# The down projection of a two-layer MLP by the seven-product form of the 2x2 block product

## The chip, the cores and the metric

The kernel runs on one core of one Trainium2 chip, as one launch. The metric is the device time of an execution in microseconds (us), the median of the runs.

## The reference

One transformer block on 256 tokens of width 1024, in float32. Attention comes first and is untouched by this change; it ends in a projection and a residual. Then comes the part that the change is about, a feed-forward block with a hidden width of 4096 (cut to what matters):

```python
def squared_relu_mlp(x, w_up, w_down):          # x 256x1024, w_up 1024x4096, w_down 4096x1024
    return jnp.square(jax.nn.relu(x @ w_up)) @ w_down

def reference(x, ...):
    h = x
    u = moba_attention(rms_norm(h, norm_mix_pre[0]), attn_w_qkv[0], attn_w_o[0])
    h = h + rms_norm(u, norm_mix_post[0])
    u = squared_relu_mlp(rms_norm(h, norm_ffn_pre[0]), w_up[0], w_down[0])
    return h + rms_norm(u, norm_ffn_post[0])
```

## The kernel before

**Split operands.** TensorE multiplies in a format (float32r) that keeps part of a float32's bits. So every operand is split exactly into a high part and a low part, and `mm3` (L209 to L214) issues three matmuls for each product: high by high, high by low, low by high. For weights the split is made on chip by the class `Weights`: ScalarE (ACT) copies a slice of the loaded `raw` tile to `hi` (L83), and VectorE (DVE) subtracts, `lo = raw - hi` (L84), with both inputs in SBUF. A few of these subtractions, outside the feed-forward block's steady part, are given to GpSimd (POOL).

**The stream of weights.** A piece is a tile of 128 x 2048 (1 MB); five raw tiles and four pairs of parts are in flight. `pump(n)` issues the next n splits (512 columns each) of a fixed list `steps`; `get` makes sure that a split needed by a matmul has been issued; `done` releases parts. When the last split of a piece has been issued, the load of a later piece is put on SyncE's (SP) queue. The order of PE and SP is the order of the program text; ACT, DVE and POOL are ordered by a list scheduler by priority, outside sections marked as manual, and each engine then runs its instructions in that fixed order.

**The feed-forward block.** The hidden width is cut into eight chunks of 512. The first chunk goes by token tiles, while the residual's norm is worked out (`up_first`). Every later chunk c is `up_chunk(c)`: four groups f of 128 hidden units, each 8 x 3 matmuls of 256 columns (tokens) into one PSUM bank `psu`; then `up_evac`: DVE takes relu times the norm to `r` (L555), ACT squares it twice, to `uhi` (L556) and `u` (L557), and DVE subtracts `ulo = u - uhi` (L558). After `up_chunk(c)` comes `down_chunk(c-1)`: 4 row blocks x 2 token tiles x 2 column halves x 3 = 48 matmuls of 512 columns into four accumulator banks `acd` that stay open over all chunks. The last chunk's down products are done by output tile, so that `PostNorm` (square on ACT, a power on POOL, the gain and the residual on DVE, L526 to L533) overlaps the next tile's matmuls.

PSUM is eight banks: pool `mm` has four (the accumulators), pool `at` four (the `psu` tiles).

Of the kernel before, what the change touches and what calls it, by code (L numbers as in the profile page):

```python
# [17 lines left out]
P = 128  # L18
# [3 lines left out]


# [4 lines left out]
class Weights:  # L28
    """Streams the weights through SBUF in pieces of [128, 2048] and splits each float32
    exactly into two float32r parts: hi (12 bits, rounded) and lo (the rest). A piece is split  # L30
    in four steps; step (i, j) is the j-th of piece i."""

    N = 2048

    def __init__(self, nc, raw_pool, part_pool, raw_bufs, part_bufs):
        self.nc, self.raw_pool, self.part_pool = nc, raw_pool, part_pool
        self.raw_bufs, self.part_bufs = raw_bufs, part_bufs
        self.sources, self.raw, self.parts, self.steps, self.split = [], {}, {}, [], set()
        self.loaded = self.finished = self.next = self.part = 0
# [23 lines left out]
    def slice(self, t, i, j):  # L63
        how = self.sources[i][1]
        if how == "cols":
            return t[:, :, j * P:(j + 1) * P]
        if how == "rows":
            return t[:, j // 2, (j % 2) * 512:(j % 2) * 512 + 512]
        return t[:, j, :]

    def pump(self, n, lo_engine=None):
        nc = self.nc
        while n > 0 and self.next < len(self.steps):
            i, j = self.steps[self.next]
            if i >= self.finished + self.part_bufs or i >= self.loaded:
                return
            if i not in self.parts:
                shape = list(self.raw[i].shape)
                self.parts[i] = [self.part_pool.tile(shape, F32R, name=f"w{p}{i}", tag=f"w{p}", bufs=self.part_bufs)
                                 for p in ("hi", "lo")]  # L80
            hi, lo = (self.slice(t, i, j) for t in self.parts[i])
            x = self.slice(self.raw[i], i, j)
            nc.scalar.activation(hi, x, AF.Copy)  # L83
            (lo_engine or nc.vector).tensor_tensor(lo, x, f32(hi), op=ALU.subtract)  # L84
            self.split.add((i, j))
            self.next += 1
            n -= 1
            if sum((i, q) in self.split for q in range(4)) == 4:
                self.load()

    def get(self, i, j):
        while (i, j) not in self.split:
# [3 lines left out]
        return self.parts[i]  # L96
# [6 lines left out]
def block(ctx: ExitStack, tc: tile.TileContext, x, g_mix_pre, g_mix_post, g_ffn_pre, g_ffn_post,  # L103
# [20 lines left out]
    # ---- the weights in the order of their use  # L124
# [7 lines left out]
    def add_cols(name, w, c, how, cuts=1):  # L132
        """512 columns in two pieces of four row blocks"""
# [7 lines left out]
    def add_rows(name, w, k):  # L141
        """four row blocks in two pieces"""
# [12 lines left out]
    NC = F // 512  # L155
    for c in range(NC):
        add_cols(f"up{c}", wu, 512 * c, "cols" if c else "k")
        if c > 0:
            add_rows(f"down{c - 1}", wd, 4 * (c - 1))
    add_rows(f"down{NC - 1}", wd, 4 * (NC - 1))  # L160

    # ---- loads: x's columns as the first weights need them
# [21 lines left out]
    # ---- constants  # L184
# [8 lines left out]
    # distances of queries 128.. to keys 0..255, then of queries 0.. to keys 0..127  # L193
    dist = const.tile([P, 384], F32, name="dist")
# [12 lines left out]
    oT = [const.tile([P, HEADS, S], F32R, name=f"oT{i}") for i in range(2)]  # L207
# [26 lines left out]
    def diag_of(rstd):  # L234
        """diagonal matrices of rstd, split in two parts"""
# [7 lines left out]
    def row_of(dg, dst, pool):  # L243
        """dst[:, t] = rstd[t] on every partition"""
# [5 lines left out]
    # ---- x transposed, times the first gain; its rows' norms come in later  # L250
# [20 lines left out]

    qk_pool = tc.alloc_tile_pool(name="qk_pool", bufs=1)
# [71 lines left out]
    # ---- attention, a head at a time; the queries of the second half come first  # L344
# [60 lines left out]
    # ---- values, queries and keys of the first heads  # L405
# [3 lines left out]
    def keep_busy(n):  # L409
        """products of zeros, which keep TensorE's clock up while it waits"""  # L410
# [73 lines left out]
    # ---- projection of the heads' outputs  # L484
# [60 lines left out]
    rrow2 = const.tile([P, S], F32, name="rrow2")  # L545
    up = {}

    def up_tiles(c):
        up[c] = [mlp.tile([P, 4, S], F32R, name=f"u{p}") for p in ("hi", "lo")]

    def up_evac(c, f, ps):
        hi, lo = (a[:, f, :] for a in up[c])
        r = mlp.tile([P, S], F32, name="r")
        u = mlp.tile([P, S], F32, name="u")
        nc.vector.scalar_tensor_tensor(r, ps[:, :S], 0.0, rrow2, op0=ALU.max, op1=ALU.mult)  # L555
        nc.scalar.activation(hi, r, AF.Square)  # L556
        nc.scalar.activation(u, r, AF.Square)  # L557
        nc.vector.tensor_tensor(lo, u, f32(hi), op=ALU.subtract)  # L558
# [11 lines left out]
    def up_first_relu(t):  # L570
        r = mlp.tile([P, 512], F32, name=f"r0_{t}", bufs=1)
        nc.vector.tensor_scalar(r, rT[t], rstd2[:, t:t + 1], 0.0, op0=ALU.mult, op1=ALU.max)
        rT[t] = r

    def up_first_evac(t):
# [3 lines left out]
        hi, lo = (a[:, :, t * P:(t + 1) * P] for a in up[0])  # L579
        u = mlp.tile([P, 4, P], F32, name=f"u0_{t}", bufs=1)  # L580
        psv = ps.rearrange("p (f c) -> p f c", c=P)
        nc.scalar.activation(hi, psv, AF.Square)
        nc.scalar.activation(u, psv, AF.Square)
        nc.vector.tensor_tensor(lo, u, f32(hi), op=ALU.subtract)
# [4 lines left out]
    with tc.manual_schedule(engines=ELEMENTWISE):  # L589
# [20 lines left out]
        up_tiles(0)  # L610
# [15 lines left out]
        for k in range(KT):  # L626
# [10 lines left out]
            if k == 6:  # L637
                row_of(dg, rrow2, at)
# [6 lines left out]
    def up_chunk(c):  # L645
        up_tiles(c)
        for f in range(4):
            ps = bank(at, f"psu{c}_{f}")
# [5 lines left out]
            if f == 3:
                W.done(2)
            W.pump(2)
            up_evac(c, f, ps)

    def down_chunk(c):
        for f in range(4):  # L660
            for t in range(NT):
                for n in range(2):
                    a = [b[:, f, t * P:(t + 1) * P] for b in up[c]]
                    rows_unit(f"down{c}", f, a, t, n, c == 0 and f == 0, False)
            if f % 2:
                W.done(1)
            W.pump(2)

    for c in range(1, NC):
        up_chunk(c)  # L670
        if c == 1:
            acc = [[bank(mm, f"acd{t}_{n}") for n in range(2)] for t in range(NT)]
        down_chunk(c - 1)
    ov = out[0].rearrange("(t p) d -> p t d", p=P)

    def act_down(f, t):
        return [b[:, f, t * P:(t + 1) * P] for b in up[NC - 1]]

    for t in range(NT):
        norm = PostNorm(t, "ffn")  # L680
        for c in range(2):
            last_rows(f"down{NC - 1}", act_down, t, c)
            norm.take(c)
        for a, b in ((0, 512), (512, D)):
            norm.put(yg, a, b)
            nc.sync.dma_start(ov[:, t, a:b], yg[:, t, a:b])
    W.done(2)
# [25 lines left out]
```

## Time and profile before

| what | value |
|---|---|
| time, median of 3 runs | 306.8 us (306.6 to 307.12) |
| span of the profiled execution, first to last instruction | 304.8 us |
| median time less that span | 2.0 us |
| PE busy | 295.1 us (97%) |
| DVE busy | 194.1 us (64%) |
| ACT busy | 166.6 us (55%) |
| POOL busy | 24.4 us (8%) |

The span is from one profiled execution; the time of a run is the device's own and holds 2.0 us that lie around the span. A matmul's duration in the trace is longer than the step from one matmul to the next, since they are pipelined; the cost of a matmul in a dense stream is therefore read from start to start.

### The profile page before, as it was taken

What the parts mean: (1) busy time and instruction counts of PE and PEld (TensorE: products, weight loads), DVE (VectorE), ACT (ScalarE), POOL (GpSimd) and SP (SyncE); (2) the same over time, 40 slices, a digit from 0 to 9 for tenths busy, and PEclk for the clock granted to TensorE, in tenths of its full rate; (3) what the DMA queues carried; (4) which work ended last, traced back from release to release, by engine and by line L of the source; (5) the groups of instructions that cost most, each with busy time, mean ns of one, the idle gap of its engine ahead of it and who ended that gap; (6) DMA issues with size and microseconds to landing.
All of it is one profiled execution on the core that took longest, in us unless ns stands there. A gap on an engine that the chain in (4) does not pass through costs nothing.

```text
span 304.8 us, 4862 instructions
## 1 busy us (share of the span) xinstructions
PE 295.1 (97%) x1838; PEld 261.9 (86%) x1838; DVE 194.1 (64%) x403; ACT 166.6 (55%) x395; POOL 24.4 (8%) x38
## 2 busy tenths in 40 slices
PE   8999999999999989999999999999999999999991
PEld 4689999988998868898898898898898898898880
DVE  3569989774688296899448447447447447547042
ACT  4777938765393365987437427427527526526020
POOL 4000224002200072000000000000000000000000
PEclk9999999999999999999999999999999999999998
DMA  6998694739405234078970860960960950300012
GB/s 201 374 387 310 205 380 172 251 133 347 141 3 166 110 138 140 0 254 293 298 261 1 310 245 0 326 226 2 336 214 9 345 199 12 129 0 3 0 57 80
DMA packets 22055, 53.79 MB, mean 176 GB/s; under 512 B 1024, under 2 KB 1552, under 8 KB 22032
## 3 DMA queue, kind: packets, MB, share of 16 engines
q1 hardware_dynamic: 22032, 53.49, 50.1%
q8 instruction: 14, 0.23, 0.3%
q14 instruction: 9, 0.07, 0.1%
HBM read 52.44 MB, written 1.05 MB: 175 GB/s over the span
## 4 chain that ended last, share of the span: by engine, by line
PE 80%; issue 10%; DVE 5%; DMA 2%; SPq 1%; ACT 1%; POOL 1%; DVEq 0%; POOLq 0%
PE psu L212 10%; PE psu L214 10%; PE psu L213 10%; PE acd L213 9%; PE acd L212 9%; PE acd L214 9%; PE psq L212 3%; PE psq L213 3%; PE psq L214 3%; DVE wlo L84 2%; PE psv L292 2%; PE psv L294 2%; PE psv L296 2%; DMA raw<-in_attn_w_qkv_dram 2%; PE psk L212 1%
## 5 line engine op out<-in xcount | busy, mean ns | idle before, releaser
L84 DVE TENSOR_TENSOR wlo<-raw,whi 128x512 fp32r<-128x512 f32 x182 | 118.3, 697 | 43.2 <-ACT whi L83 43.0
L83 ACT ACTIVATE whi<-raw 128x512 fp32r<-128x512 f32 x192 | 107.0, 623 | 46.4 <-PE acd L214 33.3
L212 PE MATMUL psu<-xT,whi 128*128 128x256 f32 x224 | 63.4, 283 | 0.0
L213 PE MATMUL psu<-xT,whi 128*128 128x256 f32 x224 | 63.3, 282 | 0.0
L214 PE MATMUL psu<-xT,wlo 128*128 128x256 f32 x224 | 62.9, 281 | 0.0
L213 PE MATMUL acd<-wlo,uhi 128*128 128x512 f32 x128 | 50.5, 395 | 0.0
L212 PE MATMUL acd<-whi,uhi 128*128 128x512 f32 x128 | 50.5, 395 | 0.0
L214 PE MATMUL acd<-whi,ulo 128*128 128x512 f32 x128 | 50.5, 394 | 0.0
L214 PEld LDWEIGHTS psu<-xT,wlo 128*128 128x128 f32 x224 | 42.5, 190 | 0.0
L213 PEld LDWEIGHTS psu<-xT,whi 128*128 128x128 f32 x224 | 42.1, 188 | 0.3
L212 PEld LDWEIGHTS psu<-xT,whi 128*128 128x128 f32 x224 | 41.9, 187 | 0.3
L556 ACT ACTIVATE uhi<-r 128x256 fp32r<-128x256 f32 x28 | 11.6, 413 | 35.0 <-DVE r L555 35.0
L214 PEld LDWEIGHTS acd<-whi,ulo 128*128 128x128 f32 x128 | 24.1, 188 | 5.6
L212 PEld LDWEIGHTS acd<-whi,uhi 128*128 128x128 f32 x128 | 24.1, 188 | 5.4
L213 PEld LDWEIGHTS acd<-wlo,uhi 128*128 128x128 f32 x128 | 24.1, 189 | 5.3
L558 DVE TENSOR_TENSOR ulo<-u,uhi 128x256 fp32r<-128x256 f32 x28 | 11.8, 423 | 14.4 <-ACT u L557 14.4
L555 DVE SCALAR_TENSOR_TENSOR r<-psu,rrow 128x256 f32<-128x256 f32 x28 | 11.7, 419 | 13.7 <-PE psu L214 13.7
L212 PE MATMUL psq<-xT,whi 128*128 128x256 f32 x64 | 18.4, 288 | 0.0
L212 PE MATMUL psk<-xT,whi 128*128 128x256 f32 x64 | 18.4, 287 | 0.0
L529 POOL TENSOR_TENSOR rs<-mss,power 128x1 f32<-128x1 f32 x4 | 2.2, 550 | 198.6 <-DVE mss L527 198.6
L214 PE MATMUL psq<-xT,wlo 128*128 128x256 f32 x64 | 18.1, 282 | 0.0
L213 PE MATMUL psq<-xT,whi 128*128 128x256 f32 x64 | 18.0, 282 | 0.0
(121 smaller groups left out, 455.2 us busy)
## 6 DMA issues: line engine op xcount, KB each, us to landing
raw<-in_w_up_dram SPq DMA_DIRECT2D x16, 1024.0 KB, 5.6
raw<-in_w_down_dram SPq DMA_DIRECT2D x16, 1024.0 KB, 7.5
raw<-in_attn_w_qkv_dram SPq DMA_DIRECT2D x10, 1024.0 KB, 8.6
raw<-in_attn_w_o_dram SPq DMA_DIRECT2D x4, 1024.0 KB, 5.7
raw<-in_attn_w_qkv_dram SPq DMA_DIRECT2D x8, 256.0 KB, 6.3
out_dram<-yg SPq DMA_DIRECT2D x4, 256.0 KB, 2.0
xs<-in_x_dram SPq DMA_DIRECT2D x2, 256.0 KB, 4.9
xs<-in_x_dram SPq DMA_DIRECT2D x1, 512.0 KB, 7.1
```

Of the source, the lines that this page charges most:

```text
L83: nc.scalar.activation(hi, x, AF.Copy)
L84: (lo_engine or nc.vector).tensor_tensor(lo, x, f32(hi), op=ALU.subtract)
L212: nc.tensor.matmul(ps, lhsT=a[0], rhs=b[0], start=start, stop=False)
L213: nc.tensor.matmul(ps, lhsT=a[0], rhs=b[1], start=False, stop=False)
L214: nc.tensor.matmul(ps, lhsT=a[1], rhs=b[0], start=False, stop=stop)
L292: nc.tensor.matmul(psv[0][t], lhsT=x0[t], rhs=w[0], start=first, stop=False)
L294: nc.tensor.matmul(psv[0][t], lhsT=x1[t], rhs=w[0], start=False, stop=False)
L296: nc.tensor.matmul(psv[0][t], lhsT=x0[t], rhs=w[1], start=False, stop=last)
L529: nc.gpsimd.tensor_tensor(self.rs, ms, power[:, :1], op=ALU.pow)
L555: nc.vector.scalar_tensor_tensor(r, ps[:, :S], 0.0, rrow2, op0=ALU.max, op1=ALU.mult)
L556: nc.scalar.activation(hi, r, AF.Square)
L558: nc.vector.tensor_tensor(lo, u, f32(hi), op=ALU.subtract)
```

## The change

Only the feed-forward block changes. The hidden width is now taken in 16 pairs q of 2 x 128 rows of `w_down`. For a pair, the two row blocks, the two token tiles and the two 512-column halves make a 2x2 block product. It needs eight block products in the plain form; fifteen of the sixteen pairs now use a seven-product form, whose operands are blocks or sums of blocks. The last pair stays plain. There are seven accumulator banks, `M1` to `M7` (four in `mm`, three in `at`), so one bank of `at` is left for `psu`; both f of a pair share it.

The sums of weights are made on POOL (`add_up`: one subtraction of 1024 columns and two of 512, into one tile `sum` with a single buffer). The sums of activations are made on POOL (`combine`: four operations of 128 columns), on DVE for pair 0. Each down piece then has two units, `blocks` (3 x 512 columns) and `sums` (4 x 512), each split into hi and lo; a split now covers 1024 columns, save one of 512. The activations of a pair are seven 128-column blocks, squared once on ACT, copied to hi by ACT and subtracted to lo by DVE (896 columns each). `down_pair(q-3)` follows `up_pair(q)`. At the end DVE combines the seven banks into four partial results, which the final norm adds to the last pair's products.

```diff
+    def add_up(self, i):
+        raw = self.raw[i]
+        t = self.sums[i] = self.sum_pool.tile([P, 4, 512], F32, name=f"sum{i}", tag="sum", bufs=1)
+        sub = self.nc.gpsimd.tensor_tensor
+        sub(t[:, 0:2, :], raw[:, :, 512:1024], raw[:, 0, :].rearrange("p (h c) -> p h c", c=512), op=ALU.subtract)
+        sub(t[:, 2, :], raw[:, 1, 512:1024], t[:, 0, :], op=ALU.subtract)
+        sub(t[:, 3, :], raw[:, 1, 0:512], t[:, 2, :], op=ALU.subtract)
+
+    def operands(self, u, j):
+        i, kind = self.units[u]
+        raw, (hi, lo) = self.raw[i], self.parts[u]
+        if kind == "blocks":
+            if j == 0:
+                return hi[:, 0, :], lo[:, 0, :], raw[:, 0, 0:512]
+            return hi[:, 1:3, :], lo[:, 1:3, :], raw[:, 1, :].rearrange("p (h c) -> p h c", c=512)
+        if kind == "sums":
+            s = slice(2 * j, 2 * j + 2)
+            return hi[:, s, :], lo[:, s, :], self.sums[i][:, s, :]
+        return tuple(self.slice(t, kind, j) for t in (hi, lo, raw))
...
     def pump(self, n, lo_engine=None):
...
+                if kind == "blocks":
+                    self.add_up(i)
+            hi, lo, x = self.operands(u, j)
             nc.scalar.activation(hi, x, AF.Copy)
             (lo_engine or nc.vector).tensor_tensor(lo, x, f32(hi), op=ALU.subtract)
...
+    for q in range(2, NP):
+        add_pair(q)
+        if q >= LAG:
+            add_down(q - LAG, "seven")
+    for q in range(NP - LAG, NP - 1):
+        add_down(q, "seven")
+    add_down(NP - 1, "rows")
...
+    A21, A11, A22, A12, S1, S3, S2, S4 = range(8)
+    PRODUCTS = (("M1", A11, 0, 0), ("M2", A12, 0, 1), ("M3", S4, 0, 2), ("M5", S1, 1, 0),
+                ("M7", S3, 1, 1), ("M6", S2, 1, 2), ("M4", A22, 1, 3))
...
+    def combine(q):
+        x = hidden.pop(q)
+        if q < NP - 1:
+            tt = (nc.vector if q == 0 else nc.gpsimd).tensor_tensor
+            tt(x[:, S1, :], x[:, A21, :], x[:, A22, :], op=ALU.add)
+            tt(x[:, S3, :], x[:, A11, :], x[:, A21, :], op=ALU.subtract)
+            tt(x[:, S2, :], x[:, S1, :], x[:, A11, :], op=ALU.subtract)
+            tt(x[:, S4, :], x[:, A12, :], x[:, S2, :], op=ALU.subtract)
+        hi, lo = (mlp.tile([P, 7, P], F32R, name=f"u{p}{q}", tag=f"u{p}", bufs=UB) for p in ("hi", "lo"))
+        src, n = (x[:, 1:8, :], 7) if q < NP - 1 else (x[:, 0:4, :], 4)
+        act[q] = hi, lo
+        nc.scalar.activation(hi[:, 0:n, :], src, AF.Copy)
+        nc.vector.tensor_tensor(lo[:, 0:n, :], src, f32(hi[:, 0:n, :]), op=ALU.subtract)
+
+    def up_evac(q, ps):
+        r = mlp.tile([P, 512], F32, name=f"r{q}", tag="r", bufs=2)
+        nc.vector.scalar_tensor_tensor(r, ps, 0.0, rrow2.rearrange("p f s -> p (f s)"), op0=ALU.max, op1=ALU.mult)
+        hidden[q] = r
+
+    def up_finish(q):
+        r = hidden[q]
+        x = hidden_tile(q)
+        nc.scalar.activation(x[:, 0:4, :], r.rearrange("p (f c) -> p f c", c=P), AF.Square)
+        combine(q)
...
-            if k > 1:
+            if k in (2, 4, 6):
                 W.pump(1)
...
+    def up_pair(q):
+        ps = bank(at, f"psu{q}")
+        for f in range(2):
             for k in range(KT):
+                w = [a[:, k, f * P:(f + 1) * P] for a in W.get(piece[f"up{q}"], k // 4)]
+                mm3(ps[:, f * S:(f + 1) * S], w, xk(k), k == 0, k == KT - 1)
+            if q == 2 and f == 1:
                 up_first_evac(1)
+                combine(0)
+                combine(1)
+            if f == 0:
+                W.pump(2)
+        W.done(1)
+        up_evac(q, ps)
+        W.pump(1)
+        up_finish(q)
...
+    def down_pair(q):
+        hi, lo = act.pop(q)
+        if q == 0:
+            for j, (name, *_) in enumerate(PRODUCTS):
+                M[name] = bank(mm if j < 4 else at, f"ac{name}")
+        for name, slot, e, j in PRODUCTS:
+            a = hi[:, slot - 1, :], lo[:, slot - 1, :]
+            w = [b[:, j, :] for b in W.get(piece[f"down{q}"] + e, j // 2)]
+            last = q == NP - 2 and name not in ("M2", "M3", "M4")
+            mm3(M[name], a, w, q == 0, last)
+            if name == "M3":
                 W.done(1)
+            if name in ("M1", "M3", "M6"):
+                W.pump(1)
+        W.done(1)
+
+    for q in range(2, NP):
+        up_pair(q)
+        if q >= LAG:
+            down_pair(q - LAG)
+    for q in range(NP - LAG, NP - 1):
+        down_pair(q)
...
+    nc.scalar.activation(part["m1"], M["M1"], AF.Copy)
+    for d, a, b in (("u2", "M6", "m1"), ("u3", "M7", "u2"), ("u4", "M5", "u2"), ("u7", "M5", "u3")):
+        nc.vector.tensor_tensor(part[d], M[a], part[b], op=ALU.add)
...
+    class FinalNorm(PostNorm):
+        def take(self, c, first):
...
+            nc.vector.tensor_tensor(yc, M[name], yc, op=ALU.add)
...
+            square(scr, yc, ss)
```

LAG is 3 and UB is 2.

## Rows read from the trace of the kernel before

**Rows 1.** The page: engines' busy time, the chain that ended last, granted TensorE clock.
```profile
PE 295.1 (97%) x1838; PEld 261.9 (86%) x1838; DVE 194.1 (64%) x403; ACT 166.6 (55%) x395; POOL 24.4 (8%) x38
...
PEclk9999999999999999999999999999999999999998
...
PE 80%; issue 10%; DVE 5%; DMA 2%; SPq 1%; ACT 1%; POOL 1%; DVEq 0%; POOLq 0%
```

**Rows 2.** Windows: us; busy of PE PEld DVE ACT POOL; clock; DMA share, GB/s.
```profile
127.93:298.40 170.47, 170.45 (x1061) 153.23 (x1059) 98.95 (x184) 84.42 (x180) 0.55 (x1) 1.00 0.45 158
177.08:199.75 22.67, 22.67 (x147) 20.56 (x146) 13.05 (x25) 11.46 (x24) 0.00 (x0) 1.00 0.55 185
```

**Rows 3.** Timeline (start us, us, engine ...) of PE: first matmuls of three stretches.
```profile
127.93 0.28 PE L212 MATMUL psu<-xT,whi 128*128 128x256 f32 x1
...
139.86 0.40 PE L212 MATMUL acd<-whi,uhi 128*128 128x512 f32 x1
...
151.01 0.28 PE L212 MATMUL psu<-xT,whi 128*128 128x256 f32 x1
```

**Rows 4.** Timeline of DVE from 185 us, operations back to back.
```profile
185.73 0.42 DVE L555 SCALAR_TENSOR_TENSOR r<-psu,rrow 128x256 f32<-128x256 f32 x1
186.08 1.29 DVE L84 TENSOR_TENSOR wlo<-raw,whi 128x512 fp32r<-128x512 f32 x2
187.29 0.42 DVE L558 TENSOR_TENSOR ulo<-u,uhi 128x256 fp32r<-128x256 f32 x1
187.63 2.49 DVE L84 TENSOR_TENSOR wlo<-raw,whi 128x512 fp32r<-128x512 f32 x4
```

**Rows 5.** Timeline of ACT from 186 us, operations back to back.
```profile
186.48 0.40 ACT L556 ACTIVATE uhi<-r 128x256 fp32r<-128x256 f32 x1
186.78 0.40 ACT L557 ACTIVATE u<-r 128x256 f32<-128x256 f32 x1
...
190.99 2.19 ACT L83 ACTIVATE whi<-raw 128x512 fp32r<-128x512 f32 x4 [2.25 <-PE acd L214]
```

**Rows 6.** Timeline of DVE, 33 to 41 us, beside POOL's subtractions.
```profile
33.21 1.89 DVE L84 TENSOR_TENSOR wlo<-raw,whi 128x512 fp32r<-128x512 f32 x3
...
35.39 1.79 DVE L84 TENSOR_TENSOR wlo<-raw,whi 128x512 fp32r<-128x512 f32 x1
...
37.44 2.97 DVE L84 TENSOR_TENSOR wlo<-raw,whi 128x512 fp32r<-128x512 f32 x3
```

**Rows 7.** Timeline of POOL, the same stretch.
```profile
35.32 1.30 POOL L84 TENSOR_TENSOR wlo<-raw,whi 128x512 fp32r<-128x512 f32 x1 [12.66 <-ACT whi L83]
37.71 1.55 POOL L84 TENSOR_TENSOR wlo<-raw,whi 128x512 fp32r<-128x512 f32 x1 [1.08 <-ACT whi L83]
```

**Rows 8.** Timeline of DVE and POOL, 109 to 118 us.
```profile
109.07 3.45 DVE L533 SCALAR_TENSOR_TENSOR xs<-yg,rs,xs 128x512 f32<-128x512 f32 x2
117.15 1.41 DVE L533 SCALAR_TENSOR_TENSOR xs<-yg,rs,xs 128x512 f32<-128x512 f32 x2
...
109.01 2.96 POOL L84 TENSOR_TENSOR wlo<-raw,whi 128x512 fp32r<-128x512 f32 x2
```

**Rows 9.** Timeline of DVE at 51.9 us, and of POOL.
```profile
51.94 0.47 DVE L359 SCALAR_TENSOR_TENSOR s<-pss,rstd_q,bias 128x256 f32<-128x256 f32 x1
...
51.98 1.29 POOL L84 TENSOR_TENSOR wlo<-raw,whi 128x512 fp32r<-128x512 f32 x1 [2.11 <-ACT whi L83]
```

**Rows 10.** Timeline of the end, from the last matmul.
```profile
297.98 0.40 PE L214 MATMUL acd<-whi,ulo 128*128 128x512 f32 x1
...
299.33 0.68 DVE L530 TENSOR_TENSOR yg<-acd,g_ffn 128x512 f32<-128x512 f32 x1
299.49 0.55 POOL L529 TENSOR_TENSOR rs<-mss,power 128x1 f32<-128x1 f32 x1 [5.09 <-DVE mss L527]
300.07 1.41 DVE L533 SCALAR_TENSOR_TENSOR yg<-yg,rs,xs 128x512 f32<-128x512 f32 x2
```

**Rows 11.** DMA issues of the up weights, KB each, median us to landing.
```profile
raw<-in_w_up_dram SPq DMA_DIRECT2D x16, 1024.0 KB, 5.6
```

More of the change, by code (lines that the diff above doesn't have):

```diff
@@ L21 @@
 MASKED = 1e30
+UB = 2
+LAG = 3
 def f32(ap):
@@ L33 @@
     N = 2048
+    STEPS = {"cols": 4, "k": 4, "rows": 4, "pair": 2, "blocks": 2, "sums": 2}
     def __init__(self, nc, raw_pool, part_pool, raw_bufs, part_bufs):
@@ L37, in __init__ @@
         self.raw_bufs, self.part_bufs = raw_bufs, part_bufs
-        self.sources, self.raw, self.parts, self.steps, self.split = [], {}, {}, [], set()
+        self.sources, self.raw, self.left = [], {}, []
+        self.units, self.parts, self.steps, self.split = [], {}, [], set()
         self.loaded = self.finished = self.next = self.part = 0
+        self.sum_pool, self.sums = None, {}
     def add(self, src, how, cuts=1):
-        self.sources.append((src, how, cuts))
-        return len(self.sources) - 1
+        kinds = ("blocks", "sums") if how == "seven" else (how,)
+        self.sources.append((src, cuts))
+        self.left.append(sum(self.STEPS[k] for k in kinds))
+        for k in kinds:
+            self.units.append((len(self.sources) - 1, k))
+        return len(self.units) - len(kinds)
     def load(self, n=None):
@@ L61, in load, with slice @@
             self.part = 0
-    def slice(self, t, i, j):
-        how = self.sources[i][1]
-        if how == "cols":
+    def slice(self, t, kind, j):
+        if kind == "cols":
             return t[:, :, j * P:(j + 1) * P]
-        if how == "rows":
+        if kind == "rows":
             return t[:, j // 2, (j % 2) * 512:(j % 2) * 512 + 512]
+        if kind == "pair":
+            return t[:, 4 * j:4 * j + 4, :]
         return t[:, j, :]
+    def add_up(self, i):
[16 more added lines that the diff above has]
+        return tuple(self.slice(t, kind, j) for t in (hi, lo, raw))
     def pump(self, n, lo_engine=None):
@@ L73, in pump, with get @@
         while n > 0 and self.next < len(self.steps):
-            i, j = self.steps[self.next]
-            if i >= self.finished + self.part_bufs or i >= self.loaded:
+            u, j = self.steps[self.next]
+            i, kind = self.units[u]
+            if u >= self.finished + self.part_bufs or i >= self.loaded:
                 return
-            if i not in self.parts:
-                shape = list(self.raw[i].shape)
-                self.parts[i] = [self.part_pool.tile(shape, F32R, name=f"w{p}{i}", tag=f"w{p}", bufs=self.part_bufs)
+            if u not in self.parts:
+                shape = {"blocks": [P, 3, 512], "sums": [P, 4, 512]}.get(kind, list(self.raw[i].shape))
+                self.parts[u] = [self.part_pool.tile(shape, F32R, name=f"w{p}{u}", tag=f"w{p}", bufs=self.part_bufs)
                                  for p in ("hi", "lo")]
-            hi, lo = (self.slice(t, i, j) for t in self.parts[i])
-            x = self.slice(self.raw[i], i, j)
+                if kind == "blocks":
+                    self.add_up(i)
+            hi, lo, x = self.operands(u, j)
             nc.scalar.activation(hi, x, AF.Copy)
             (lo_engine or nc.vector).tensor_tensor(lo, x, f32(hi), op=ALU.subtract)
-            self.split.add((i, j))
+            self.split.add((u, j))
             self.next += 1
             n -= 1
-            if sum((i, q) in self.split for q in range(4)) == 4:
+            self.left[i] -= 1
+            if self.left[i] == 0:
                 self.load()
-    def get(self, i, j):
-        while (i, j) not in self.split:
+    def get(self, u, j):
+        while (u, j) not in self.split:
             n = self.next
@@ L95, in get @@
             assert self.next > n
-        return self.parts[i]
+        return self.parts[u]
     def done(self, n):
@@ L154, in block, with add_pair, add_down @@
     add_rows("o1", wo, 4)
[L155 to L160, printed above, removed]
+    NP = F // 256
+    add_cols("up0", wu, 0, "k")
+    def add_pair(q):
+        i = piece[f"up{q}"] = W.add(wu[:, :, 256 * q:256 * q + 256], "pair")
+        W.steps += [(i, j) for j in range(2)]
+    def add_down(q, how):
+        i = piece[f"down{q}"] = W.add(wd[:, 2 * q:2 * q + 2, :], how)
+        W.steps += [(i, j) for j in range(4)] if how == "rows" else [(i + e, j) for e in range(2) for j in range(2)]
+    for q in range(2, NP):
[5 more added lines that the diff above has]
+    add_down(NP - 1, "rows")
     xs = const.tile([P, NT, D], F32, name="xs")
@@ L206, in block @@
     xT = [const.tile([P, KT, S], F32R, name=f"xT{i}") for i in range(2)]
-    oT = [const.tile([P, HEADS, S], F32R, name=f"oT{i}") for i in range(2)]
+    oT = [o_pool.tile([P, HEADS, S], F32R, name=f"oT{i}") for i in range(2)]
     def mm3(ps, a, b, start, stop):
@@ L511, in block @@
     yg = mlp.tile([P, NT, D], F32, name="yg", bufs=1)
+    W.sum_pool = mlp
     class PostNorm:
@@ L544, in block, with hidden_tile @@
     rstd2 = const.tile([P, NT], F32, name="rstd2")
[L545 to L558, printed above, removed]
+    rrow2 = const.tile([P, 2, S], F32, name="rrow2")
+    A21, A11, A22, A12, S1, S3, S2, S4 = range(8)
+    PRODUCTS = (("M1", A11, 0, 0), ("M2", A12, 0, 1), ("M3", S4, 0, 2), ("M5", S1, 1, 0),
+                ("M7", S3, 1, 1), ("M6", S2, 1, 2), ("M4", A22, 1, 3))
+    hidden, act = {}, {}
+    def hidden_tile(q):
+        hidden[q] = mlp.tile([P, 8, P], F32, name=f"x{q}", tag="x", bufs=2)
+        return hidden[q]
+    @urgent
+    def combine(q):
[11 more added lines that the diff above has]
+        nc.vector.tensor_tensor(lo[:, 0:n, :], src, f32(hi[:, 0:n, :]), op=ALU.subtract)
+    @urgent
+    def up_evac(q, ps):
[7 more added lines that the diff above has]
+        combine(q)
     rT = {}
@@ L578, in up_first_evac @@
             nc.tensor.transpose(ps[:, f * P:(f + 1) * P], rT[t][:, f * P:(f + 1) * P], ident)
[L579 to L584, printed above, removed]
+        for q in range(2):
+            x = hidden[q] if t else hidden_tile(q)
+            psv = ps[:, q * 256:(q + 1) * 256].rearrange("p (f c) -> p f c", c=P)
+            nc.scalar.activation(x[:, 0:4, :].rearrange("p (f t) c -> p f t c", t=2)[:, :, t, :], psv, AF.Square)
     def act_o(f, t):
@@ L637, in block @@
             if k == 6:
-                row_of(dg, rrow2, at)
+                row_of(dg, rrow2[:, 0, :], at)
+                nc.gpsimd.tensor_copy(rrow2[:, 1, :], rrow2[:, 0, :])
             if k % 4 == 3:
                 W.done(1)
-            if k > 1:
+            if k in (2, 4, 6):
                 W.pump(1)
         up_first_relu(1)
[L645 to L648, printed above, removed]
+    o_pool.release()
+    late = ctx.enter_context(tc.tile_pool(name="late", bufs=1, side="right", reuse_waits="tile"))
@@ L653, in up_chunk @@
                 up_first_evac(1)
[L654 to L665, printed above, removed]
-                W.done(1)
[L667 to L673, printed above, removed]
@@ new lines, in block @@
+    M["C22"] = bank(at, "acC22")
+    result = {(0, 0): ("M4", "u3"), (0, 1): ("C22", "u7"), (1, 1): ("M3", "u4"), (1, 0): ("M2", "m1")}
+    hi, lo = act.pop(NP - 1)
+    class FinalNorm(PostNorm):
+        def take(self, c, first):
+            s = slice(c * 512, (c + 1) * 512)
+            name, rest = result[self.t, c]
+            yc = part[rest]
+            nc.vector.tensor_tensor(yc, M[name], yc, op=ALU.add)
+            scr = small.tile([P, 512], BF16, name="scr", bufs=2)
+            ss, ms = self.ss[:, c:c + 1], self.ms[:, c:c + 1]
+            square(scr, yc, ss)
+            nc.vector.tensor_scalar(ms, ss, EPS if first else self.ms[:, 1 - c:2 - c], None, op0=ALU.add)
+            if not first:
+                nc.gpsimd.tensor_tensor(self.rs, ms, power[:, :1], op=ALU.pow)
+            (nc.gpsimd if first or self.t == 0 else nc.vector).tensor_tensor(
+                yg[:, self.t, s], yc, self.gain[:, s], op=ALU.mult)
@@ new lines, in block @@
+    for t in range(NT):
+        norm = FinalNorm(t, "ffn")
+        order = (0, 1) if t == 0 else (1, 0)
+        for n, c in enumerate(order):
+            name = result[t, c][0]
+            for f in range(2):
+                a = [b[:, 2 * f + t, :] for b in (hi, lo)]
+                w = [b[:, f, c * 512:(c + 1) * 512] for b in W.get(piece[f"down{NP - 1}"], 2 * f + c)]
+                mm3(M[name], a, w, f == 0 and name == "C22", f == 1)
+            norm.take(c, n == 0)
+        for c in order:
+            norm.put(yg, c * 512, (c + 1) * 512)
+            nc.sync.dma_start(ov[:, t, c * 512:(c + 1) * 512], yg[:, t, c * 512:(c + 1) * 512])
@@ L691 @@
+    W.done(1)
 _INS = ["x", "norm_mix_pre", "norm_mix_post", "norm_ffn_pre", "norm_ffn_post", "w_up", "w_down",
```

26 lines of the change are left out of this document (8 added, 18 removed).

## The prediction

> **What bounds the kernel now.** I read the page first: PE is busy for 97% of the span and fills 80% of the chain that ended last, DVE is at 64%, ACT at 55%, and POOL, at 8%, is nearly idle; the granted clock is full until the end [rows 1]. So the first guess is that fewer matmuls mean less time. The windows then show the feed-forward block by itself: from 127.93 to 298.40 PE is busy for 170.45 of 170.47 us, and POOL for 0.55 [rows 2]. One chunk of 512 hidden units takes 22.67 us, of which DVE works 13.05 and ACT 11.46 [rows 2]. That leaves DVE some 9.6 us a chunk, or 4.8 a pair. Whether the change fits into that room is the question, and averages over the span don't answer it.
>
> **What it takes from PE.** In the PE timeline the 48 down matmuls of a chunk run from 139.86 to 151.01, so a 512-column matmul costs 11.15 / 48 = 0.2323 us from start to start; the remaining 11.52 us of a 22.67 us chunk are 96 matmuls of 256 columns, 0.120 each [rows 2, 3]. Plain, a pair has 8 x 3 = 24 down matmuls; in the seven-product form 21. Fifteen pairs save 45, or 45 x 0.2323 = 10.45 us. The up matmuls keep their number and shape. A pair then asks of PE 48 x 0.120 + 21 x 0.2323 = 10.64 us, against 11.33 before.
>
> **What it adds to DVE.** Back to back, two 512-column subtractions take 186.08 to 187.29, 0.605 each, and a 256-column operation 185.73 to 186.08, 0.35 [rows 4]. So 256 more columns cost 0.255, and by that line a 1024-column subtraction costs 0.605 + 0.51 = 1.115 and an 896-column one 0.99. Per pair: two up splits 2.23; blocks 0.605 + 1.115 = 1.72; sums 2.23; the activations' lo 0.99; relu of 512 columns 0.605. Together 7.78 us. The upper bound, if the longer operations gain nothing over 512-column ones, is 7040 columns / 512 x 0.605 = 8.32. Alone, DVE would still be done within PE's 10.64.
>
> **ACT.** A 512-column copy costs 2.19 / 4 = 0.55, a 256-column one 0.30 [rows 5], so 1024 columns cost about 1.05 and 896 about 0.92. Per pair five of 1024, one copy and one square of 512, one of 896: 7.3 us, hidden under PE. The copy to a pair's activation parts has to wait for a free buffer (UB is 2) until the down products of two pairs before are done; the weight copies that those products need have to stand ahead of it on ACT, or nothing would move, so I cost that wait at nothing.
>
> **What it adds to POOL, and what that does to DVE.** This is the term that decides. Per pair POOL gets subtractions of 1024, 512 and 512 columns and four of 128, all with both inputs in SBUF. The trace has POOL subtractions of 512 columns: 1.30 us undisturbed [rows 7]. Beside them, look at DVE. Three of its subtractions alone take 1.89 us [rows 6]. The one that starts at 35.39, just behind POOL's of 35.32, takes 1.79 and ends 0.56 us after POOL's end at 36.62. The three from 37.44 take 2.97, and POOL's, issued at 37.71 into the first of them, stretches to 1.55 [rows 6, 7]. From 109.07 two residual operations of DVE (again two SBUF inputs) take 3.45 us beside POOL's; later, without POOL, two take 1.41 [rows 8]. So the two engines take turns: while one runs an operation with two SBUF inputs, the other's waits. A DVE operation with only one input in SBUF, at 51.94, keeps its 0.47 us beside a POOL subtraction [rows 9]; relu, which reads PSUM, is of that kind, the splits aren't. The extra time that one POOL subtraction of 512 columns puts on DVE is 1.79 - 0.61 = 1.18, 2.97 - 1.89 = 1.08, or (3.45 - 1.41) / 2 = 1.02; the mean is 1.09.
>
> The Trainium skill says the same of the mechanism (SBUF — State Buffer, "Who interferes with whom"): a DVE instruction with two SBUF inputs contends with a GpSimd instruction that reads SBUF, and the second to issue blocks until the first is done. By that rule, taken with POOL's whole 1.29 us, the sum below would come to 357 us; by the measured delays it is the lower figure that follows.
>
> No row shows POOL at 1024 columns. I take two times the price of 512 (four units in all, 4 x 1.09 = 4.36 us a pair); at least it is 4 x 1.02, at most POOL's whole time, 4 x 1.29. For 128 columns the bounds are a quarter of 1.02, 0.255, and 0.55, the smallest POOL operation with two tensors that I have (a power on one column) [rows 10]; between them I take 0.40, so 1.6 for four.
>
> So in the steady state DVE needs, working or held up, 7.78 + 4.36 + 1.6 = 13.74 us a pair: more than PE's 10.64, and more than the 11.33 of before. DVE becomes the bound, and PE waits some 3 us in each pair for the lo parts of the sums. Low bound: 4 x 1.02 + 4 x 0.255 = 5.1, with relu run during POOL's turns (7.78 - 0.605), 12.3. High: 8.32 + 4 x 1.29 + 4 x 0.55 = 15.7.
>
> **The sum.** The stretch begins at 127.93, where PE starts the first chunk that goes by column groups [rows 3]. Fifteen pairs of DVE time: 15 x 13.74 = 206.1. Corrections: only 14 up pairs, -2.84; pair 0's activation sums run on DVE (4 x 0.22, by the line above) and not on POOL, -0.73; three up splits are issued before the stretch, -3.35; the last pair's lo, 512 columns, +0.61: -6.3 in all. After the last lo of sums PE still has four products of the last seven-product pair, 12 x 0.2323 = 2.79, and the plain pair, 24 x 0.2323 = 5.58. The end behind the last matmul was 304.8 - 298.4 = 6.4 us, and gets one more DVE addition ahead of the square, 0.68 as its neighbour in that chain [rows 10]: 7.1. Span: 127.93 + 206.1 - 6.3 + 2.79 + 5.58 + 7.1 = 343.2; with the 2.0 that lie between span and median, **345.2 us**. The bounds of a pair's time give 323 and 374. The same formula gives 306.8 at 11.18 us a pair: the change pays only if POOL holds DVE for less than 3.4 us a pair.
>
> **Edits costed at nothing.** The up weights now come in rows of 1 KB and not 2: if that doubled the DMA engines' work on them, the share of 0.55 over a chunk would be 0.83 [rows 2], and a load that lands in 5.6 us [rows 11] has five buffers; covered. The single psu bank has to be emptied during the 4.9 us of down matmuls behind it; one relu of 0.6 fits, even behind one held-up subtraction of 2 to 3.5. The four combining additions on DVE (2.7 us) run under the last 24 matmuls.
>
> **Rivals.**
> - *POOL's work stays off DVE's path.* If these plain float32 sums hold DVE up far less than the splits on POOL did (under 2.9 us a pair), PE stays the bound and the matmuls saved are the result: 306.8 - 10.45 + 0.68 = 297.0 us. For it: PE's 97%, and DVE and POOL each alone fit into 10.64. Against: three separate stretches show the turns, with two kinds of DVE operation. It decides at 3.4 us. Chance 0.15.
> - *Part of the price.* Half of it gives 10.8 us a pair, 301. Chance 0.03.
> - *Waits in fixed queues on top.* `sum` has one buffer, so POOL may start the next pair's sums only after DVE's last lo of this one; then ACT (1.05) and DVE (1.115) follow POOL's last subtraction. If POOL has nothing else in that time, 2.17 us are added to a pair: 15.9, 378 us. Against: `combine` and the up splits can fill it. Chance 0.06.
> - *TensorE's clock falls in the waits.* It stayed at 1.00 through this stretch [rows 2], but PE never waited there. At half clock a pair would take 21.3 us of PE, 458 us; a few slow stretches would vanish in PE's new slack. Chance 0.02.
>
> My own case has the rest, 0.74. Slower by over 0.2% (about what a measurement of this kernel can tell from no change) then is 0.82, faster 0.17, within 0.2% 0.01. The range, 312 to 376, holds my case's bounds of 323 to 374, most of what lies between a partial price and them, and part of the queue rival; together about 0.8.
>
> **What would show it.** In the profile after: DVE's 1024-column subtractions at a mean well above 1.2 us, near 2; POOL busy for some 100 us in the block; DVE's busy share near 1 there; PE's share down to about 83%, its waits put down to DVE's `wlo`; the period of a pair near 13.7 us and the chain led by DVE and POOL. If a pair takes 10.6 us and PE stays dense, the step on POOL's price is wrong.

## The result, and the profile after

The changed kernel takes 337.6 us (median of 4 runs, 337.17 to 338.59) against 306.8: a ratio of 1.100 (95% interval 1.098 to 1.102). Predicted were 345.2 us, 312 to 376. The 45 matmuls fewer did not come back as time: a pair of the down projection now takes 12.7 us, where half a chunk took 11.33.

The page of the changed kernel, the lines of [rows 1]: engines' busy time, granted clock, and the chain that ended last.

```profile
PE 298.6 (89%) x1793; PEld 262.5 (78%) x1793; DVE 286.0 (85%) x356; ACT 187.1 (56%) x342; POOL 204.8 (61%) x143
...
PEclk9999999999999799999599997999799999899595
...
POOL 54%; PE 31%; DVE 8%; issue 3%; ACT 2%; DMA 1%; POOLq 0%; DVEq 0%
```

PE has left the chain's first place to POOL. DVE has fewer instructions than before (356 against 403) and is busy for 92 us more: the instructions themselves have become longer. In part they cover more columns, but the groups by shape (count, then busy us and mean ns) show that this isn't all: a split of 1024 columns takes 2.26 us in the mean where the raw blocks are split, against 1.22 without POOL's sums (the run with all sums on DVE, below).

```profile
L122 DVE TENSOR_TENSOR wlo<-raw,whi 128x1024 fp32r<-128x1024 f32 x43 | 96.1, 2258 | 0.0
L122 DVE TENSOR_TENSOR wlo<-sum,whi 128x1024 fp32r<-128x1024 f32 x30 | 43.5, 1481 | 2.3 <-ACT whi L121 2.3
```

The windows, with columns as in [rows 2], show where: the block's beginning, its steady part, and two single pairs.

```profile
140.00:160.00 20.00, 18.55 (x114) 16.09 (x113) 16.24 (x13) 10.87 (x13) 19.61 (x15) 1.00 0.45 151
...
160.00:260.00 100.00, 89.76 (x543) 80.83 (x544) 100.00 (x65) 55.72 (x64) 98.11 (x57) 0.93 0.54 169
...
199.66:212.38 12.72, 11.89 (x68) 11.09 (x69) 12.72 (x10) 6.96 (x8) 12.48 (x8) 0.87 0.50 167
212.38:225.13 12.75, 11.34 (x71) 9.63 (x70) 12.75 (x9) 6.96 (x8) 12.51 (x8) 1.00 0.53 164
```

From 160 to 260 us DVE and POOL are both busy all the time. Two engines can't both be the bound by their own work; here each one's busy time holds its waiting for the other. The timeline of DVE over one pair of the changed kernel (start us, us, ...) shows it, to be held against [rows 4]:

```profile
207.64 4.81 DVE L122 TENSOR_TENSOR wlo<-raw,whi 128x1024 fp32r<-128x1024 f32 x2
212.38 0.68 DVE L632 SCALAR_TENSOR_TENSOR r<-psu,rrow 128x512 f32<-128x512 f32 x1
212.98 3.41 DVE L122 TENSOR_TENSOR wlo<-raw,whi 128x512 fp32r<-128x512 f32 x2
216.31 2.88 DVE L122 TENSOR_TENSOR wlo<-sum,whi 128x1024 fp32r<-128x1024 f32 x2
219.12 1.35 DVE L627 TENSOR_TENSOR ulo<-x,uhi 128x896 fp32r<-128x896 f32 x1
220.39 4.82 DVE L122 TENSOR_TENSOR wlo<-raw,whi 128x1024 fp32r<-128x1024 f32 x2
```

And POOL's, the same kernel, to be held against [rows 7]:

```profile
208.00 3.38 POOL L90 TENSOR_TENSOR sum<-raw 128x1024 f32<-128x1024 f32 x1
211.45 2.15 POOL L91 TENSOR_TENSOR sum<-raw,sum 128x512 f32<-128x512 f32 x1
213.68 1.62 POOL L92 TENSOR_TENSOR sum<-raw,sum 128x512 f32<-128x512 f32 x1
215.26 1.45 POOL L619 TENSOR_TENSOR x<-x 128x128 f32<-128x128 f32 x1
...
220.75 3.38 POOL L90 TENSOR_TENSOR sum<-raw 128x1024 f32<-128x1024 f32 x1
```

Two splits of 1024 columns take 4.74 us from start to start (207.64 to 212.38) beside POOL's 1024-column subtraction, and the two of the sums only 2.81, beside POOL's short operations. Relu, which has one input in PSUM, takes 0.60 from start to start (212.38 to 212.98), in the midst of POOL's subtraction from 211.45 to 213.60; it isn't held up. POOL's 128-column operations are stretched most of all, to 1.45 us: each has to wait for a DVE split of 1024 columns to end. Alone, one takes 0.46 (at 154.56, where DVE waits for ACT):

```profile
154.56 0.46 POOL L619 TENSOR_TENSOR x<-x 128x128 f32<-128x128 f32 x1
```

### The profile page after: what moved, and what is told of

It reads as the page before. It is cut to its first block, busy times and chain, and to the rows that moved or that the text cites. A ratio compares the mean times of both kernels' runs of the same rounds, so it can differ in the third digit from the quotient of the medians.

```text
span 335.3 us, 4825 instructions
## 1 busy us (share of the span) xinstructions
PE 298.6 (89%) x1793; PEld 262.5 (78%) x1793; DVE 286.0 (85%) x356; ACT 187.1 (56%) x342; POOL 204.8 (61%) x143
## 2 busy tenths in 40 slices
DMA packets 29223, 53.79 MB, mean 160 GB/s; under 512 B 1024, under 2 KB 15888, under 8 KB 29200
## 4 chain that ended last, share of the span: by engine, by line
POOL 54%; PE 31%; DVE 8%; issue 3%; ACT 2%; DMA 1%; POOLq 0%; DVEq 0%
POOL sum L90 14%; POOL sum L91 9%; POOL sum L92 8%; POOL x L620 6%; POOL x L621 6%; POOL x L619 5%; POOL x L622 5%; DVE wlo L122 4%; PE psv L344 2%; PE psq L266 2%; PE psq L268 2%; PE psq L267 2%; PE psv L346 2%; PE psv L348 2%; PE acc L267 1%
## 5 line engine op out<-in xcount | busy, mean ns | idle before, releaser
L122 DVE TENSOR_TENSOR wlo<-raw,whi 128x512 fp32r<-128x512 f32 (+1 forms) x124 | 157.3, 1305 | 12.7 <-ACT whi L121 12.7
L121 ACT ACTIVATE whi<-raw 128x512 fp32r<-128x512 f32 (+1 forms) x134 | 94.9, 761 | 19.3 <-issue 8.9
L266 PE MATMUL psu<-xT,whi 128*128 128x256 f32 x224 | 67.4, 301 | 17.3 <-DVE r L632 17.3
L90 POOL TENSOR_TENSOR sum<-raw 128x1024 f32<-128x1024 f32 x15 | 47.6, 3171 | 19.6 <-ACT oT L271 17.2
L268 PE MATMUL acM<-whi,ulo 128*128 128x512 f32 x111 | 44.9, 405 | 4.1 <-DVE ulo L627 4.1
L122 DVE TENSOR_TENSOR wlo<-sum,whi 128x1024 fp32r<-128x1024 f32 x30 | 43.5, 1481 | 2.3 <-ACT whi L121 2.3
L267 PE MATMUL acM<-wlo,uhi 128*128 128x512 f32 x111 | 44.6, 402 | 0.8 <-DVE wlo L122 0.8
L266 PE MATMUL acM<-whi,uhi 128*128 128x512 f32 x111 | 44.8, 403 | 0.1
L121 ACT ACTIVATE whi<-sum 128x1024 fp32r<-128x1024 f32 x30 | 31.5, 1055 | 19.2 <-POOL sum L92 12.4
L91 POOL TENSOR_TENSOR sum<-raw,sum 128x512 f32<-128x512 f32 x15 | 31.1, 2074 | 1.2
L92 POOL TENSOR_TENSOR sum<-raw,sum 128x512 f32<-128x512 f32 x15 | 25.3, 1689 | 1.2
L627 DVE TENSOR_TENSOR ulo<-x,uhi 128x896 fp32r<-128x896 f32 (+1 forms) x16 | 22.5, 1404 | 3.8 <-ACT uhi L626 3.8
```

Of the source, the lines that this page charges most:

```text
L90: sub(t[:, 0:2, :], raw[:, :, 512:1024], raw[:, 0, :].rearrange("p (h c) -> p h c", c=512), op=ALU.subtract)
L91: sub(t[:, 2, :], raw[:, 1, 512:1024], t[:, 0, :], op=ALU.subtract)
L92: sub(t[:, 3, :], raw[:, 1, 0:512], t[:, 2, :], op=ALU.subtract)
L266: nc.tensor.matmul(ps, lhsT=a[0], rhs=b[0], start=start, stop=False)
L267: nc.tensor.matmul(ps, lhsT=a[0], rhs=b[1], start=False, stop=False)
L268: nc.tensor.matmul(ps, lhsT=a[1], rhs=b[0], start=False, stop=stop)
```

## The experiments

**All sums on DVE.** The direct test: the same sums, the same buffers, another engine.

```diff
-        sub = self.nc.gpsimd.tensor_tensor
+        sub = self.nc.vector.tensor_tensor
...
-            tt = (nc.vector if q == 0 else nc.gpsimd).tensor_tensor
+            tt = nc.vector.tensor_tensor
```

> All sums, of weights and of activations, are made on DVE; POOL has nothing left in the steady part. Theory of turns (an operation of DVE with two SBUF inputs waits while POOL subtracts, and the other way round): DVE's own work grows by 1.115 + 2 x 0.605 for the weight sums and 4 x 0.22 for the activation sums, to 10.98 us a pair, but the 4.95 us for which it is held up in each pair of the changed kernel go, so a pair takes about 11.0 us in place of 12.7, and the time falls from 337.6 by 15 x 1.76 to about 311 us. Rival, that the changed kernel is slow for its buffers and fixed queues (one buffer for the sums, one PSUM bank for the up products, emptied late by DVE): these are all still there, and DVE has more to do, so the time stays at 335 us or more.

Measured: 309.2 us (ratio to before 1.008, 1.005 to 1.012). DVE has more to do and the kernel is 28 us faster than with POOL's help. Two pairs in its windows:

```profile
200.12:211.29 11.17, 10.91 (x69) 9.29 (x68) 11.11 (x16) 6.85 (x8) 0.00 (x0) 1.00 0.60 188
211.29:222.31 11.02, 11.02 (x73) 9.93 (x72) 11.02 (x16) 6.85 (x8) 0.00 (x0) 1.00 0.61 192
```

A pair takes 11.0 to 11.2 us, the 10.98 of the sum; DVE is still the bound, now by its own work alone.

**Only the weight sums on DVE** (the first of the two edits above).

> Only the weight sums go to DVE; the activation sums stay on POOL. Theory of turns: weight sums cost DVE 2.33 us of its own a pair in place of 4.1 us of waiting, about 1.75 us a pair less, so about 311 us. Rival, buffers and queues: 335 us or more.

Measured: 311.8 us. As by turns in the time, but not in every pair: POOL doesn't always get the next turn. Here its first short operation waits for 9.13 us, while eight further subtractions of DVE pass at their own lengths, and comes through beside relu, which doesn't take part in the turns (POOL, then the last DVE operations of that stretch):

```profile
189.74 9.13 POOL L619 TENSOR_TENSOR x<-x 128x128 f32<-128x128 f32 x1 [6.90 <-ACT x L638]
...
195.07 2.35 DVE L122 TENSOR_TENSOR wlo<-raw,whi 128x1024 fp32r<-128x1024 f32 x2
197.34 1.22 DVE L90 TENSOR_TENSOR sum<-raw 128x1024 f32<-128x1024 f32 x1
198.48 0.69 DVE L632 SCALAR_TENSOR_TENSOR r<-psu,rrow 128x512 f32<-128x512 f32 x1
```

**Only the activation sums on DVE** (the second edit).

> Only the activation sums go to DVE; the weight sums stay on POOL. Theory of turns: four operations of 128 columns cost DVE 0.87 us of its own a pair; on POOL they hold it up for about 0.85 us (the subtractions beside them are longer by 0.2 to 0.35 each). So no change, 337 us within 3. Rival, that it is POOL's own length of work that sets the pace: POOL's four operations are 5.5 us of 12.7 in each pair, and without them a pair would take 7.2 us of POOL and PE would be the bound again, near 300 us.

Measured: 334.3 us, 3.4 under the changed kernel and so 0.4 beyond what I gave it; the rival's 300 is far off. Taking 128-column operations from POOL gains next to nothing though POOL was busy with them for 5.5 us a pair: those 5.5 us were mostly waiting.

**No weight sums.** The splits take the raw blocks instead; POOL is idle.

```diff
-                if kind == "blocks":
-                    self.add_up(i)
...
-            return hi[:, s, :], lo[:, s, :], self.sums[i][:, s, :]
+            x = raw.rearrange("p k (h c) -> p (k h) c", c=512)
+            return hi[:, s, :], lo[:, s, :], x[:, s, :]
```

> The weight sums are left out: the second unit of a pair splits the raw blocks again, in the same sizes, so its output is not the reference's. Activation sums on DVE. Everything else, the matmuls, the splits, the buffers, the single PSUM bank, stays. Theory of turns: DVE needs 7.78 + 0.87 = 8.65 us a pair, PE 10.64, so PE is the bound and the time is about 297 to 300 us. Rival, buffers and queues: PE still waits on the bank that DVE empties, 320 us or more.

Measured: 300.3 us (0.980, 0.975 to 0.984), at the edge of what was expected. PE is dense in its window, and a pair takes the 10.64 us worked out for PE (200.24 to 210.88, the same split of two pairs, in DVE's timeline below the window's row). So the single PSUM bank, the two buffers of activations and the order of the queues cost nothing in the steady part by themselves:

```profile
160.00:260.00 100.00, 100.00 (x647) 91.18 (x646) 82.20 (x111) 65.35 (x76) 0.00 (x0) 1.00 0.58 196
...
200.24 2.36 DVE L121 TENSOR_TENSOR wlo<-raw,whi 128x1024 fp32r<-128x1024 f32 x2
...
210.88 2.36 DVE L121 TENSOR_TENSOR wlo<-raw,whi 128x1024 fp32r<-128x1024 f32 x2
```

**POOL works, but reads nothing.** POOL keeps its place in the chain and fills the tile of the sums with counts.

```diff
-        sub = self.nc.gpsimd.tensor_tensor
...
+        for j in range(4):
+            for _ in range(2):
+                self.nc.gpsimd.iota(t[:, j, :], pattern=[[1, 512]], base=0, channel_multiplier=1,
+                                    allow_small_or_imprecise_dtypes=True)
```

> In place of the three subtractions that make the weight sums, POOL writes the same tile with eight counts (iota) of 512 columns, which read nothing from SBUF; so the sums are wrong and so is the output. Activation sums on DVE. POOL is busy for some 5 us a pair, and the splits of the sums wait for it as before. Theory of turns, with reading SBUF as what they take turns at: DVE isn't held up, the time is that of the kernel without weight sums, 300 us. Rival, that any POOL work holds DVE up, or that the order through POOL and the single buffer is what costs: 320 us or more.

Measured: 300.7 us. Its timeline, POOL and then DVE beside it:

```profile
200.34 4.13 POOL L91 IOTA sum<- 128x512 f32 x8 [6.51 <-DVE wlo L122]
...
201.20 2.35 DVE L122 TENSOR_TENSOR wlo<-raw,whi 128x1024 fp32r<-128x1024 f32 x2
```

POOL writes to SBUF for 4.13 us without a break, and two DVE splits of 1024 columns beside it keep their 2.35. So neither POOL's being busy, nor its writes, nor the dependency of the splits on POOL holds DVE up.

**POOL works and reads one input.** The same, with a scaling of the raw block:

```diff
+                self.nc.gpsimd.tensor_scalar(t[:, j, :], x[:, j, :], 0.5, 1.0, op0=ALU.mult, op1=ALU.mult)
```

> The same with eight scalings of 512 columns, each with one SBUF input, in place of the counts (the sums are wrong, and so is the output). Theory of turns at reading SBUF: a scaling of 384 columns took 0.51 to 0.54 us before, so one of 512 about 0.7, and eight hold DVE up for 4 to 5.5 us a pair; 8.65 + 4.0 to 5.5 is 12.7 to 14.2, so 335 to 355 us. Rival, that only POOL operations with two inputs hold DVE up: 300 us.

Measured: 320.8 us. The mechanism came out, its size did not: I had taken the scaling's whole duration.

```profile
200.09 3.17 DVE L122 TENSOR_TENSOR wlo<-raw,whi 128x1024 fp32r<-128x1024 f32 x2
203.19 0.68 DVE L632 SCALAR_TENSOR_TENSOR r<-psu,rrow 128x512 f32<-128x512 f32 x1
203.79 2.62 DVE L122 TENSOR_TENSOR wlo<-raw,whi 128x512 fp32r<-128x512 f32 x2
206.34 0.69 DVE L619 TENSOR_TENSOR x<-x 128x128 f32<-128x128 f32 x1
...
211.66 3.18 DVE L122 TENSOR_TENSOR wlo<-raw,whi 128x1024 fp32r<-128x1024 f32 x2
```

Two splits of 1024 columns take 3.10 from start to start, not 2.23 to 2.27: 0.41 to 0.43 for each scaling of 512 columns, against 1.09 for a subtraction. A pair takes 11.57 us from 200.09 to 211.66. POOL's operations with one input hold DVE up too, for less than half as long.

**Late norm, all sums on DVE.** The token's norm multiplies all hidden units of a token, so it can be taken out and left to the last norm, with an epsilon scaled per token. The diff shows the norm's part; the sums are moved as in the first experiment. Relu is then a plain floor at zero, which ACT does from PSUM.

```diff
-        nc.vector.scalar_tensor_tensor(r, ps, 0.0, rrow2.rearrange("p f s -> p (f s)"), op0=ALU.max, op1=ALU.mult)
+        nc.scalar.activation(r, ps, AF.Relu)
...
-        nc.vector.tensor_scalar(r, rT[t], rstd2[:, t:t + 1], 0.0, op0=ALU.mult, op1=ALU.max)
+        nc.vector.tensor_scalar(r, rT[t], 0.0, None, op0=ALU.max)
...
+        nc.vector.scalar_tensor_tensor(ms, ssq2[:, 0, t:t + 1], EPS, ssq2[:, 1, t:t + 1], op0=ALU.add, op1=ALU.add)
+        nc.vector.scalar_tensor_tensor(eps2[:, t:t + 1], ms, EPS, ms, op0=ALU.mult, op1=ALU.mult)
...
-            nc.vector.tensor_scalar(ms, ss, EPS if first else self.ms[:, 1 - c:2 - c], None, op0=ALU.add)
+            nc.vector.tensor_scalar(ms, ss, eps2[:, self.t:self.t + 1] if first else self.ms[:, 1 - c:2 - c], None, op0=ALU.add)
```

> All sums on DVE; and the token's norm, which multiplies every hidden unit, is left out of the hidden units and taken into the last norm instead (the last norm divides it out again, but for its epsilon, which is scaled per token). So relu is a plain copy with a floor at zero, and ACT does it from PSUM. DVE: 10.98 - 0.60 = 10.38 us a pair, ACT 7.3 + 0.55, PE 10.64. Theory: PE is the bound again, as in the kernel without weight sums, 300 to 303 us, faster than both kernels. Rival, that a DVE filled to 98% leaves PE waiting at every pair for its fixed order: 305 us or more.

Measured: 298.6 us (0.975, 0.973 to 0.977); a second time 298.5 (0.974, 0.971 to 0.976). Faster than both kernels, and 1.4 us better than I gave it; why, no run shows. In this window PE and DVE are both busy throughout, and no wait of PE's is left in the block:

```profile
160.00:260.00 100.00, 100.00 (x650) 91.62 (x649) 100.00 (x136) 69.51 (x86) 0.00 (x0) 1.00 0.61 198
```

The kernel before was not run with the late norm, so what part of the 2.5% it would have given there is not shown. PE was already busy there for 170.45 of the block's 170.47 us.

**Late norm, sums on POOL.** In the changed kernel PE waits for relu; this is the whole of that wait in the waits of PE there (us in total, times, longest):

```profile
PE psu L266 <- DVE r L632: 17.3, 10, 3.7
```

So relu alone was taken off DVE, with the sums left on POOL (the edit of the late norm, without that of the first experiment).

> The changed kernel with its sums on POOL, and with the late norm alone: relu, and with it the emptying of the one PSUM bank of the up products, goes from DVE to ACT. In the changed kernel PE waits 17.3 us for relu (ten times). Theory of turns: DVE is the bound; it loses 0.60 us of its own a pair (9 us in all), but in that time POOL could run, so a pair falls by between nothing and 0.60 us: 328 to 337 us. PE's waits move to other releasers. Rival, that the single bank and relu's place in DVE's queue are a cause of their own: PE's 17.3 us go, 320 us or less.

Measured: 337.5 us, no change. PE's wait has moved to others (the waits of PE, and the timeline of DVE over a pair):

```profile
PE psu L266 <- ACT r L636: 7.4, 8, 0.9
PE acM L267 <- DVE wlo L122: 7.1, 13, 0.6
```

```profile
206.51 7.92 DVE L122 TENSOR_TENSOR wlo<-raw,whi 128x1024 fp32r<-128x1024 f32 x4
214.36 3.71 DVE L122 TENSOR_TENSOR wlo<-sum,whi 128x1024 fp32r<-128x1024 f32 x2
217.99 1.35 DVE L631 TENSOR_TENSOR ulo<-x,uhi 128x896 fp32r<-128x896 f32 x1
219.26 7.91 DVE L122 TENSOR_TENSOR wlo<-raw,whi 128x1024 fp32r<-128x1024 f32 x4
```

A pair still takes 12.75 us, from 206.51 to 219.26. DVE's own work with two SBUF inputs is 7.17 us of it, so POOL's turns are 5.58. Relu's 0.60 us had been free, inside POOL's turns; what is scarce here isn't DVE's time but the turn.

**The end.** Last, the late-norm kernel with the gain's multiplications moved off POOL.

```diff
-            (nc.gpsimd if first or self.t == 0 else nc.vector).tensor_tensor(
+            nc.vector.tensor_tensor(
```

> The kernel with the late norm and all sums on DVE, and at the end the gain's multiplications on DVE too, not on POOL. In that kernel 10.4 us pass from the last matmul's end to the end of the span, 6.4 before the change: POOL takes 3.75 us for three multiplications, its power stands behind them in its queue, and DVE's residual behind the power. If that order is what costs, the power comes some 2.5 us earlier, while DVE has about 1.8 us more to do: 0.5 to 2.5 us less than the same kernel beside it. If DVE's own work at the end is what sets it, no change or 1 us more.

> The same kernel as late_norm, beside the one with the other end: about 298.6 us.

Measured: 298.4 and 298.5 us: no change. With the gain on DVE, POOL's first power starts 0.2 us after the last matmul's end and not 1.9, but the last residual on DVE starts 5.2 us after it and not 5.4: DVE has more to do ahead of the second power, for which that residual waits. Where the longer end of the seven-product form comes from was not taken further.

## Why the prediction was right, and where its sum was off

- **The deciding step held.** POOL's subtractions and DVE's splits take turns, so what the change puts on POOL is paid on DVE. Removing POOL's reads (all sums on DVE, no weight sums, counts in place of subtractions) takes 28 to 37 us off; removing other suspects (relu and the bank, POOL's short operations) takes 0 to 3.4. The prediction's row for an operation of relu's kind, at 51.94, had not shown that POOL leaves it alone, since it started before POOL's; the changed kernel's relu at 212.38 does. The section of the Trainium skill quoted in the prediction (SBUF — State Buffer, "Who interferes with whom") also says that a GpSimd instruction which only writes SBUF is not met, nor is GpSimd met by a DVE instruction with at most one SBUF input, outside DVE's 2-port modes. The counts (300.7 us) and relu's being free agree. "At most one input" is not the whole rule, though: in the kernel before, a DVE operation with one SBUF input took 1.39 us beside a POOL subtraction while the other seven of its line and shape have a mean of 0.29 (DVE, POOL, and the group of all eight):

```profile
48.57 1.39 DVE L366 TENSOR_SCALAR s<-s,st 128x128 f32<-128x128 f32 x1
...
48.58 1.29 POOL L84 TENSOR_TENSOR wlo<-raw,whi 128x512 fp32r<-128x512 f32 x1
...
L366 DVE TENSOR_SCALAR s<-s,st 128x128 f32<-128x128 f32 x8 | 3.4, 428 | 0.0
```

- **What PE gives back was right in a pair, and too much in all.** With POOL's weight sums gone and PE dense, a pair takes the 10.64 us of the sum. But 300.3 to 300.7 us were measured where the sum for a PE-bound kernel was 297.0: without the weight sums, 10.3 us pass from the last matmul's end to the end of the span (288.19 to 298.5), where the sum had 7.1.
- **The price of a pair was 1.0 us too high**, 13.74 against 12.74, or 15 us over 15 pairs. Two terms: relu, 0.60, was counted on DVE's path, and the last experiment but one shows it inside POOL's turns (the low bound had it so). And POOL's turns came to 5.57 and not 5.96. Of these the short ones are the part I had least for: beside the sums' splits (2.81 for two, 2.27 without POOL) and the activations' (1.27 for 1.00) they cost 0.27 each, near the low bound of 0.255, not 0.40.
- **The ends were 7.4 us too short.** Subtracting 15 x 12.74 from 337.6 leaves 146.5, where the sum had 139.1. From 127.93 to the end of the last lo of sums, at 316.29, 188.4 us pass, where 15 x 12.74 - 6.3 gives 184.8. DVE idles for 6.1 of them: 3.8 of the 20 us from 140, waiting through POOL and ACT for its first activations, and 2.3 ahead of 305.59, where ACT's copy had to wait for the last subtraction of that pair's sums on POOL (the queue rival's wait, seen here once and not in each pair). Its other work there is 2.5 us shorter than the sum has it. From the last lo to the last matmul's end 9.0 us pass (to 325.33), not 8.4; the first matmuls there are still 0.43 us apart, not 0.23. After it 10.0 pass, not 7.1, and the median lies 2.3 above the profiled span, not 2.0. Together 7.4. The two errors have opposite signs: 345.2 less 15.0 plus 7.4 is the 337.6 measured, so part of the nearness of the forecast is luck.

```profile
305.59 1.23 DVE L122 TENSOR_TENSOR wlo<-sum,whi 128x1024 fp32r<-128x1024 f32 x1 [2.28 <-ACT whi L121]
...
312.73 3.56 DVE L122 TENSOR_TENSOR wlo<-sum,whi 128x1024 fp32r<-128x1024 f32 x2
...
324.93 0.40 PE L268 MATMUL acM<-whi,ulo 128*128 128x512 f32 x1
```

- **Where PE waits was wrong.** I costed the single PSUM bank at nothing, covered by the down matmuls, and expected the waits at the sums' lo parts. In the changed kernel 17.3 us of them stand at relu, which is behind held-up splits in DVE's queue. It is a place, not a cause: with relu off DVE the time stays. Two of the signs were also off: from 127.93 to 328.40 POOL is busy for 176 us and not for some 100, since its busy time holds its waiting, and PE's share of the span is 89%, not 83%.
- **The clock's rival** was right in kind: the granted clock falls in some of the stretches where PE waits, to 0.87 over the first of the pairs shown. It costs little, as PE has slack: that pair takes 12.72 us, the next, at full clock, 12.75.

## What to carry to other kernels

Before giving elementwise work to an engine that looks idle, find a stretch of the trace where it works beside the engine that you want to relieve, and price the work by what it adds to that one: here a subtraction of 512 columns that costs DVE 0.605 us cost it about 1.09 on POOL. When two engines are both near 100% busy with instructions longer than they are alone, look for waiting inside the instructions; here the trace showed no wait for it, and the mean duration by shape was where to see it. A form that trades matmuls for elementwise work pays only when the elementwise engine still ends inside PE's new, shorter time; here that took the sums on DVE and relu on ACT, by the late norm, and then the whole was worth 2.5%.

## What the runs showed of the hardware that I had not expected

- In the changed kernel's steady part the turns alternate, one operation each: POOL's 128-column operation (0.46 us alone) takes 1.44 to 1.45, as long as one of the two splits of 1024 columns beside it. They don't always. With the weight sums on DVE one such operation waited for 9.13 us; with only the activation sums there, POOL's 1024-column subtraction of a pair takes 5.43 us (205.22 to 210.65), while two DVE splits pass undisturbed in 2.35, and comes through beside relu, at 208.34. What decides who gets the next turn, no run shows.
- A POOL scaling of 512 columns with one SBUF input holds DVE's two-input operations up for 0.41 to 0.43 us, a subtraction with two for about 1.1, a count that only writes for nothing.
